# Loading the last groups of a streamed weight in other pieces: units of 16, 8, 4, 2, 1, 1 groups, whole but for the last

## The chip, the cores and the metric

One core of a Trainium2 chip. The metric is the device time of one execution in microseconds (us). Runs that are compared alternate on the same chip. Each trace is one execution; where a number is from one trace, the text says so.

## The reference

```python
# x [32, 256], y [32, 256], weight [128, 256, 256], all fp32
def reference(x, y, weight):
    return np.einsum('bi,bj,kij->bk', x, y, weight)
```

The weight is 33.55 MB and is used once. The rest is small.

## The kernel before

The 128 values of k are cut into 32 groups: group g has k = g, g+32, g+64, g+96. On one SBUF partition a group has eight rows of 256 values (a slice `ic` of i), which lie together in memory: 8 KiB of fp32. A load casts them to bf16, so that it writes 4 KiB for each partition and group. For each group, or two groups at once, TensorE adds eight matmuls (one for each `ic`) in PSUM, and VectorE multiplies by y and sums. Groups are worked on in units, and the table `LOADS` says which groups and which rows (from, to) each load brings, in the order of the queue.

```python
UNITS = (
    tuple(range(0, 32, 2)),      # 16 groups
    tuple(range(1, 32, 4)),      # 8
    (3, 11, 19, 27),
    (7, 23),
    (15, 31),
)
LOADS = (
    ((8, 24), 0, 8),
    ((4, 12, 20, 28), 0, 8),
    (tuple(range(2, 32, 4)), 0, 8),
    (tuple(range(1, 32, 4)), 0, 8),
    ((3, 11, 19, 27), 0, 8),
    ((7, 23), 4, 8),
    ((7, 23), 0, 4),
    ((15, 31), 0, 3),
    ((15, 31), 3, 5),
    ((15, 31), 5, 6),
    ((15,), 6, 8),
    ((31,), 6, 7),
    ((31,), 7, 8),
)
...
    for n, ((groups, lo, hi), s) in enumerate(zip(LOADS, s_w)):
        pool.dma_start(
            out=w_of(groups)[:, :, lo * J:hi * J],
            in_=rows_of(groups)[:, :, lo * J:hi * J],
        ).then_inc(s, 16)
...
    for u, unit in enumerate(UNITS):
        # matmuls of the unit, row by row; each waits for the load of its rows
        # then, on VectorE: one product and one sum for the unit
        # (the last unit: a fused product and sum for each group)
```

Groups 0 and 16 come as fp32 over another queue and are cast by ScalarE. All other loads of the weight are issued in the first 14 us and wait in one queue.

## Time and profile before

| | before |
|---|---|
| time, median of 3 (lowest, highest) | 86.06 us (86.01, 86.32) |
| span in the trace | 84.6 us |
| DMA, as the page's chain has it | 43% of the span, and the waits near the end |
| last piece of the weight has landed | 82.24 us |
| packets on the weight's queue | 5200 |

The page's slices (40 of 2.1 us, busy tenths) tell which engine is full at each time. The chain of work that ended last tells what set the end: a line of it is a start, a length and what ran or was waited for. The table of stretches gives, for a stretch of time, the busy time of each engine, TensorE's clock, the mean share of busy DMA engines and GB/s written. The prediction shows these lines.

Two more records are read below. A load adds 1 to its semaphore from each of the 16 DMA engines, so the trace has 16 times for each load: the middle one (between the eighth and the ninth) tells where the stream is, and I call the time from there to the sixteenth the **lag**. The packet records have a start, a size and a duration; a packet that took over 15 ns more than the usual time of its size (324 ns for 4096 bytes written, 173 for 2048, 98 for 1024, 60 for 512) I call **stretched**.

### The profile page before, as it was taken

The page shows a single profiled execution, that of the slowest core. Times are in us where ns is not written, and L with a number is a line of the kernel's source. Part 1 is how long each engine was busy: PE and PEld are TensorE (multiplying, and loading weights), DVE is VectorE, ACT ScalarE, POOL GpSimd, SP SyncE. Part 2 cuts the span into 40 slices and gives each one's busy share as a digit, 9 for nine tenths or more (in the row PEclk, how much of TensorE's full clock was granted, in tenths as well). Part 3 has the DMA queues.
Part 4 walks back from the last instruction along what each step waited for, and adds up shares of the span by engine and source line. Part 5 has one row for each costly group of instructions (what it writes and reads, how often), then busy time and mean ns, then how long its engine had stood idle before and what let it go on. Part 6 is the DMA issues. An engine that isn't in the chain of part 4 may idle for free.

```text
span 84.6 us, 277 instructions
## 1 busy us (share of the span) xinstructions
PE 32.4 (38%) x136; PEld 3.6 (4%) x38; DVE 24.9 (29%) x28; ACT 5.3 (6%) x5; POOL 10.7 (13%) x19
## 2 busy tenths in 40 slices
PE   0000000000000000000199999991079996985650
PEld 0000000000000000000000000000000010211110
DVE  0799600000000000000000000008999305999322
ACT  0638600000000000000000000000000000000000
POOL 0599994000000000000000000000000000000000
PEclk9999999999999999999999999999965999999995
DMA  4999999999999999999999999999999999999940
GB/s 112 387 411 258 211 213 217 215 213 217 213 215 211 215 217 217 215 217 215 211 215 217 215 213 217 215 215 215 209 217 217 217 215 202 208 206 207 187 53 8
DMA packets 5728, 17.91 MB, mean 212 GB/s; under 512 B 416, under 2 KB 1632, under 8 KB 5472
## 3 DMA queue, kind: packets, MB, share of 16 engines
q0 software_dynamic: 5200, 15.73, 94.5%
q1 hardware_dynamic: 432, 2.11, 6.6%
q10 hardware_dynamic: 96, 0.07, 0.3%
HBM read 33.62 MB, written 0.02 MB: 398 GB/s over the span
## 4 chain that ended last, share of the span: by engine, by line
DMA 43%; PE 38%; DVE 6%; another core or an unknown queue 4%; POOL 2%; issue 2%; POOLq 0%
DMA w_sb<-in_weight_dram 43%; PE ps L224 38%; DVE tmp L285 5%; POOL w_sb L150 1%; DVE tmp L294 0%; POOL ident L156 0%; POOL ident L155 0%; POOLq L134 0%; DVE acc L294 0%
## 5 line engine op out<-in xcount | busy, mean ns | idle before, releaser
L224 PE MATMUL ps<-w_sb,xblk 128*128 128x512 bf16 (+1 forms) x136 | 32.4, 393 | 50.3 <-DMA w_sb<-in_weight_dram 45.6
L285 DVE TENSOR_TENSOR tmp<-ps,y 128x4096 f32<-128x4096 f32 (+3 forms) x4 | 8.6, 2152 | 51.8 <-PE ps L224 51.8
L150 POOL DMA_DIRECT2D w_sb<-in_weight_dram x13 | 10.0, 778 | 2.6 <-POOLq L134 2.6
L289 DVE TENSOR_REDUCE acc<-tmp 128x16 f32<-128x4096 f32 (+3 forms) x4 | 8.6, 2154 | 0.1
L224 PEld LDWEIGHTS ps<-w_sb,xblk 128*128 128x128 bf16 x38 | 3.6, 100 | 78.7 <-DMA w_sb<-in_weight_dram 46.1
L165 ACT CAST w_sb<-w_f 128x1024 bf16<-128x1024 f32 x4 | 4.0, 1042 | 2.0 <-DMA w_f<-in_weight_dram 2.0
L294 DVE CUSTOM_DVE_ANT_0 tmp<-ps,y 128x256 f32<-128x256 f32 x2 | 0.8, 423 | 3.2 <-PE ps L224 3.2
L185 DVE STREAM_TRANSPOSE xt<-x_rep 32x256 f32<-32x256 f32 x4 | 1.7, 435 | 0.1
L214 DVE STREAM_TRANSPOSE y<-y_rep 32x256 f32<-32x256 f32 x4 | 1.7, 435 | 0.1
L197 DVE TENSOR_SCALAR xblk<-xt,mask 128x256 bf16<-128x256 f32 x4 | 1.5, 522 | 0.0
L179 DVE COPY x_rep<-x_sb 32x1024 f32<-32x1024 f32 x1 | 0.7, 681 | 2.6 <-PEq L134 2.6
L165 ACT ACT_TABLE_LOAD x1 | 1.3, 1283 | 2.6 <-PEq L134 2.6
L209 DVE COPY y_rep<-yt 32x1024 f32<-32x1024 f32 x1 | 0.7, 695 | 0.0
L206 DVE STREAM_TRANSPOSE yt<-y_sb 32x256 f32<-32x256 f32 x1 | 0.4, 422 | 0.0
L192 DVE TENSOR_REDUCE mask<-ident 128x4 f32<-128x128 f32 x1 | 0.4, 375 | 0.1
L156 POOL TENSOR_SCALAR_AFFINE_SELECT ident<-ident 128x128 f32<-128x128 f32 x1 | 0.3, 287 | 0.1
L155 POOL MEMSET ident<- 128x128 f32 x1 | 0.2, 223 | 0.0
L294 DVE DVE_READ_ACCUMULATOR2_ANT acc<- 128x1 f32 x2 | 0.2, 81 | 0.0
L324 POOL MEMSET const-float32-0.0<- 128x1 f32 x1 | 0.1, 98 | 0.2 <-issue 0.2
L324 POOL MEMSET const-bfloat16-1.0<- 128x1 bf16 x1 | 0.1, 102 | 0.0
L324 POOL MEMSET const-uint8-127<- 128x1 uint8 x1 | 0.1, 102 | 0.0
L324 POOL MEMSET const-float32-1.0<- 128x1 f32 x1 | 0.1, 98 | 0.0
## 6 DMA issues: line engine op xcount, KB each, us to landing
w_sb<-in_weight_dram POOLq DMA_DIRECT2D x2, 4096.0 KB, 46.1
w_sb<-in_weight_dram POOLq DMA_DIRECT2D x2, 2048.0 KB, 41.1
w_f<-in_weight_dram SPq DMA_DIRECT2D x2, 1024.0 KB, 6.3
w_sb<-in_weight_dram POOLq DMA_DIRECT2D x1, 1024.0 KB, 9.7
w_sb<-in_weight_dram POOLq DMA_DIRECT2D x2, 512.0 KB, 66.2
w_sb<-in_weight_dram POOLq DMA_DIRECT2D x1, 384.0 KB, 68.3
w_sb<-in_weight_dram POOLq DMA_DIRECT2D x1, 256.0 KB, 69.0
w_sb<-in_weight_dram POOLq DMA_DIRECT2D x2, 128.0 KB, 69.3
```

Source lines behind the costliest of these rows:

```text
L150: pool.dma_start(out=w_of(groups)[:, :, lo * J:hi * J], in_=rows_of(groups)[:, :, lo * J:hi * J],).then_inc(s, 16)
L165: c = act.copy(out=w_sb[:, place_of[g], lo:hi], in_=w_f[:, n, lo:hi])
L179: t = done(v.tensor_copy(out=x_rep, in_=x_sb.rearrange("b (ip ic) -> b ic ip", ic=IC).unsqueeze(3) .to_broadcast([B, IC, IP, KK]),)._wait_ ...
L185: c = v.transpose(out=xt[q * 32:(q + 1) * 32, :, :], in_=x_rep[:, :, q * IP // Q:(q + 1) * IP // Q, :],)
L192: t = done(v.tensor_reduce(out=mask, in_=ident.rearrange("p (ip kk) -> p kk ip", kk=KK), axis=AX, op=add,)._wait_ge(s_pool, 2))
L197: c = v.tensor_scalar(out=xblk[:, :, :, kk], in0=xt, scalar1=mask[:, kk:kk + 1], scalar2=None, op0=mult,)
L209: t = done(v.tensor_copy(out=y_rep, in_=yt.unsqueeze(3).to_broadcast([B, J // 32, B, KK]),)._wait_ge(s_dve, t))
L214: c = v.transpose(out=y4[q * 32:(q + 1) * 32, :].rearrange("p (jb j) -> p jb j", j=32), in_=y_rep[:, :, q * BQ:(q + 1) * BQ, :],)
L224: return pe.add_instruction(mybir.InstMatmult(name=nc.get_next_instruction_name(), engine=mybir.EngineType.PE, ins=[pe.lower_ap(rhs), pe.l ...
L285: t = done(v.tensor_tensor(out=prod, in0=sums, in1=y4.unsqueeze(1).to_broadcast([P, n_g, J]), op=mult,)._wait_ge(s_pe, n_pe))
L289: done(v.tensor_reduce(out=acc[:, unit[0]:unit[-1] + 1:unit[1] - unit[0]], in_=prod, axis=AX, op=add,)._wait_ge(s_dve, t))
L294: done(v.tensor_tensor_reduce(out=prod[:, n, :], in0=sums[:, n, :], in1=y4, scale=1.0, scalar=0.0, op0=mult, op1=add, accum_out=acc[:, g:g ...
```

## The change

Its intent: fewer and larger pieces at the end of the stream. Groups 7 and 23 come whole in one load. The pair (15, 31), which came in interleaved pieces, becomes two units: group 15 whole, and only group 31 in pieces, of 4, 2, 1 and 1 rows, so that little work is left after the last landing.

```diff
 UNITS
     (7, 23),
-    (15, 31),
+    (15,),
+    (31,),
 LOADS
-    ((7, 23), 4, 8),
-    ((7, 23), 0, 4),
-    ((15, 31), 0, 3),
-    ((15, 31), 3, 5),
-    ((15, 31), 5, 6),
-    ((15,), 6, 8),
+    ((7, 23), 0, 8),
+    ((15,), 0, 8),
+    ((31,), 0, 4),
+    ((31,), 4, 6),
     ((31,), 6, 7),
     ((31,), 7, 8),
 ... in the loop over units
-        n_b = n_g if last else n_g // 2
+        n_b = (n_g + 1) // 2
-        steps = [(ic, h, n_g // n_b * h) for ic in order for h in range(n_b)]
-        if last:
-            steps = steps[:12] + [(6, 0, 0), (7, 0, 0), (6, 1, 1), (7, 1, 1)]
+        steps = [(ic, h) for ic in order for h in range(n_b)]
-        if not last:
+        if n_g > 1:
             ... one product and one sum for the unit
         else:
-            for n, g in enumerate(unit):
-                ... fused product and sum of group g
+            ... fused product and sum of the unit's only group
 ... (bank and buffer places cut)
```

More of the change, by code (lines that the diff above doesn't have):

```diff
@@ L64 @@
     place_of = {g: i for i, g in enumerate(places)}
-    assert sorted(places) == list(range(G)) and len(UNITS[-1]) == 2 and B == 32
+    assert sorted(places) == list(range(G)) and len(UNITS[-1]) == 1 and B == 32
     def sbuf(name, shape, dtype):
@@ L241 @@
         n_g = len(unit)
-        last = u == len(UNITS) - 1
-        n_b = n_g if last else n_g // 2
+        n_b = (n_g + 1) // 2
         if bank + n_b > BANKS:
@@ L252 @@
         order = range(IC) if up else range(IC - 1, -1, -1)
-        steps = [(ic, h, n_g // n_b * h) for ic in order for h in range(n_b)]
-        if last:
-            steps = steps[:12] + [(6, 0, 0), (7, 0, 0), (6, 1, 1), (7, 1, 1)]
-        for n_step, (ic, h, o) in enumerate(steps):
+        steps = [(ic, h) for ic in order for h in range(n_b)]
+        for n_step, (ic, h) in enumerate(steps):
             n = n_g // n_b
+            o = n * h
             need = []
@@ L275 @@
                 c._wait_ge(need[-1], 16)
-            if n_step == len(steps) - 1 or (last and n_step == len(steps) - 3):
+            if n_step == len(steps) - 1:
                 n_pe += 1
                 c.then_inc(s_pe, 1)
-        prod = tmp[:, u % 2, :n_g, :]
-        if last:
-            sums = ps[:, bank:bank + n_g, 0, :]
-        else:
-            sums = ps[:, bank:bank + n_b, :, :].rearrange("p a h j -> p (a h) j")
-        if not last:
+        at = len(UNITS[1]) + u if n_g == 1 else 0
+        prod = tmp[:, u % 2 if n_g > 1 else 1, at:at + n_g, :]
+        sums = ps[:, bank:bank + n_b, :, :].rearrange("p a h j -> p (a h) j")[:, :n_g, :]
+        if n_g > 1:
             t = done(v.tensor_tensor(
@@ L292 @@
         else:
-            for n, g in enumerate(unit):
-                done(v.tensor_tensor_reduce(
-                    out=prod[:, n, :], in0=sums[:, n, :], in1=y4, scale=1.0, scalar=0.0,
-                    op0=mult, op1=add, accum_out=acc[:, g:g + 1],
-                )._wait_ge(s_pe, n_pe - 1 + n))
+            done(v.tensor_tensor_reduce(
+                out=prod[:, 0, :], in0=sums[:, 0, :], in1=y4, scale=1.0, scalar=0.0,
+                op0=mult, op1=add, accum_out=acc[:, unit[0]:unit[0] + 1],
+            )._wait_ge(s_pe, n_pe))
         bank += n_b
```

## The prediction

> **What bounds the kernel now.** I read the page's slices and queues first, then the chain of work that ended last, then a table of stretches cut at the landings of the last loads, and last the semaphore and packet records of the trace. The page of the kernel before has these lines (the span in 40 slices of 2.1 us; then the queue that carries the weight):
>
> ```profile
> PE   0000000000000000000199999991079996985650
> DMA  4999999999999999999999999999999999999940
> GB/s 112 387 411 258 211 213 217 215 213 217 213 215 211 215 217 217 215 217 215 211 215 217 215 213 217 215 215 215 209 217 217 217 215 202 208 206 207 187 53 8
> q0 software_dynamic: 5200, 15.73, 94.5%
> HBM read 33.62 MB, written 0.02 MB: 398 GB/s over the span
> ```
>
> The DMA engines are full from slice 1 to slice 37. The 215 GB/s count bytes written: the loads narrow fp32 to bf16, so the weight is read at twice that. TensorE starts halfway through and has holes. The time is therefore the time to stream 32 groups of 1 MiB, plus a short end. The chain confirms it for the end (start in us, length, what it was; "unknown queue" is the wait for a load):
>
> ```profile
> 71.36 4.48 PE ps L224 x20
> 75.83 0.46 another core or an unknown queue
> 76.29 0.05 issue
> ...
> 77.37 0.80 another core or an unknown queue
> ...
> 79.03 0.55 another core or an unknown queue
> ...
> 80.80 0.70 another core or an unknown queue
> 81.50 0.05 issue
> 81.55 0.63 PE ps L224 x3
> 82.18 0.06 another core or an unknown queue
> 82.24 0.05 issue
> 82.29 0.37 PE ps L224
> 82.66 0.02 issue
> 82.69 0.42 DVE tmp L294
> ```
>
> TensorE finishes what it has before the next piece lands, again and again, down to the last: the last piece lands at 82.24 us, and 2.36 us of fixed work (one matmul, one VectorE reduction, the store) follow to 84.6. So only the landing time of the last bytes matters. The table of stretches (window, us, busy times, TensorE clock, DMA share, GB/s written) shows that the stream slows before it ends:
>
> ```profile
> 61.50:71.30 9.80, 8.71 (x32) 0.78 (x7) 5.36 (x3) 0.00 (x0) 0.00 (x0) 0.83 1.06 213
> 71.30:76.30 5.00, 4.48 (x20) 0.97 (x10) 4.97 (x3) 0.00 (x0) 0.00 (x0) 1.00 1.13 209
> 76.30:78.20 1.90, 1.04 (x4) 0.31 (x4) 1.86 (x3) 0.00 (x0) 0.00 (x0) 1.00 1.17 204
> 78.20:79.60 1.40, 0.81 (x6) 0.19 (x2) 0.78 (x2) 0.00 (x0) 0.00 (x0) 1.00 1.32 191
> 79.60:80.40 0.80, 0.61 (x4) 0.19 (x2) 0.00 (x0) 0.00 (x0) 0.00 (x0) 1.00 1.26 180
> 80.40:80.80 0.40, 0.39 (x2) 0.10 (x1) 0.00 (x0) 0.00 (x0) 0.00 (x0) 1.00 1.38 163
> 80.80:82.20 1.40, 0.63 (x3) 0.21 (x3) 0.22 (x1) 0.00 (x0) 0.00 (x0) 1.00 0.24 31
> ```
>
> Whole groups go at 213 to 215, half groups at 209, three rows at 204, then 191, 180, 163. The last line is another thing: for 1.4 us only a quarter of the engines' time is used (0.24) while the kernel still waits. Some of the 16 engines are done and a few are late.
>
> **What the Trainium skill says.** "DMA: Bandwidth & Descriptors", section "Why small descriptors are slow (HBM only)", gives every packet a fixed overhead besides its bytes. The trace agrees that there is one: the median packet of 4096, 2048, 1536, 1024 and 512 written bytes took 324, 173, 135, 98 and 60 ns, which is about 22 ns plus 75 ns per KiB. Most of the 22 ns overlaps the next packet, since the share of busy engines is above 1 (1.06 to 1.38). The same page, section "Why a DMA increments its semaphore by 16 and not by 1", says that only the full 16 means that all has landed. The trace has 16 increments for each load, so the kernel pays the slowest engine every time; section "Latency and other measured facts" says that two of the engines are usually slower. The trace shows one increment always about 0.1 us behind the rest, but more than that at the end, below. "Rules for kernel authors" there asks for at least 1 MiB per DMA at full rate; here pieces of 128 KiB still come 0.36 us apart, because they are queued ahead.
>
> **The change part by part.** *Instructions.* The order of the built programs shows the same 120 matmuls of 512 columns, 16 of 256, and the same VectorE operations. Two DMA issues fewer (11 for 13) cost GpSimd 2 x 0.71 us (the median issue), all over by 13.7 us, long before they matter. Loads up to group 28, landed at 71.32, are untouched.
>
> *Packets.* One packet is one row piece of one group on one partition. Before, the last 4 groups took 512 + 768 + 384 = 1664 data packets, in 9 loads (the two halves of groups 7 and 23; three loads over two groups; three over one). After it is 256 + 128 + 4 x 128 = 896 in 6 loads. So 768 fewer, 48 per DMA engine. What 48 are worth comes from the time of the median engine. I take the middle of the 16 increments of each load: 71.03 (group 28), then 73.50, 75.97, 77.85, 79.16, 79.82, 80.46, 80.82, 81.18. The steps are 2.47 and 2.47 us (1 MiB in half groups), 1.88 (0.75 MiB), 1.31 (0.5 MiB), 0.66 (0.25 MiB in one-row packets), 0.64 (0.25 MiB in two-row packets), 0.36, 0.36 (0.125 MiB each). Sum 10.15. A MiB in whole rows takes 2.44: from 41.70 to 61.22 there are 8 of them. After: groups 7 and 23 whole, 2 x 2.44 = 4.88; group 15, 2.44; four rows of group 31, half of 2.47, 1.24; two rows, 0.64; one row twice, 0.72. Sum 9.92. **Saved on the median engine: 0.23 us**, on the path in full, since the chain ends in this stream.
>
> *The late engines.* The 16th increment lags the middle one by 0.28 us for the loads ending at 61.50 and 71.32, and by 0.32 at 78.17. Then 0.42, 0.54, 1.04, 1.03, 1.06 for the last five. So 0.76 us of the end is a lag that grew between 78.2 and 81.5. The packet records show where: between 79.3 and 79.9 us sixteen packets of 512 bytes took 87 to 246 ns instead of 60, and between 80.2 and 80.8 six of 1024 bytes took 251 to 405 instead of 98. Five increments slipped 0.4 us, and three of those slipped a further 0.4. Nothing in the trace names a cause. Nine packets of 2048 bytes were stretched likewise at 72.4 to 73.0 with no lasting lag. It happens where packets are small, and after the change each engine has 24 packets of at most 1024 bytes where it had 56 (16 + 16 + 8 + 8 + 8). I choose that half of the lag goes, 0.76 / 2 = 0.38, as a guess between nothing and all; a stretched packet among the last three pieces still hits.
>
> *TensorE and VectorE.* Two groups now start 8 matmuls at one landing instead of 4 and 4. With the saved time groups 7 and 23 land at about 76.2; their 8 matmuls take 8 x 0.224 (4.48 / 20) = 1.8 us, to 78.0. Group 15 lands at 78.6 and takes 8 x 0.135 (0.81 / 6) = 1.1, to 79.7. Group 31's first four rows land near 79.9, so TensorE waits again, and does them in 0.54. VectorE: product and sum of groups 7 and 23, 0.68 + 0.69, done by 79.5; one reduction of 0.42 + 0.08 for group 15, done by 80.3, before the last at 81.6. So neither joins the path, with about 0.2 us to spare at group 31's start and more later, as 1.1 us of matmul is left against 1.7 of stream. After the last landing the same 2.36 us follow.
>
> Sum: 0.23 + 0.38 = 0.6 us off 86.06, so **85.5 us**.
>
> **The rivals.** (1) *The lag stays:* the stretched packets come from something other than small packets, or the last three pieces alone bring them. For it: three of the five lagging loads keep their shape. Then 0.23 is saved, 85.8; and if the lag is worse, 86.1. (2) *The lag goes wholly:* 0.23 + 0.76 = 1.0, so 85.1. For it: loads of whole rows have kept to 0.28 throughout. Against it: the last three pieces are small still. (3) *TensorE becomes the bound*, because group 15's first matmul now waits for all eight rows. The sums above speak against it. A throttle would have to halve the clock over the last units: the page shows one such stretch of 3.4 us, before 66 us, and a second after 82. It would cost some 1 us of delay on work with 0.2 to 0.6 us of slack: at worst about 86.4. (4) *Hidden anyway*: if fewer packets freed nothing, because the memory side and not the packets limits the stream, 86.06 stays. The falling rates, 213 to 163, speak against it.
>
> **Range and chances.** The range runs from rival 2 with a little luck, 85.0, to the full lag with no gain, 86.05. A gain of 2% is 1.72 us; all that could be won is 0.39 (10.15 less 9.76) from packets and 0.76 from lag, 1.15 us, so faster has 2 in 100. Slower needs rival 3 doubled: 1 in 100.
>
> **What would show each step right or wrong.** Right: 4400 packets on the weight's queue (5200 less 768 and less 2 x 16 completions); groups 7 and 23 landing near 76.2 and group 15 near 78.7 to 78.8; a rate near 213 GB/s until then; last landing near 81.6, one matmul, one reduction, the store. Packet step wrong: the middle increments from group 28's landing to the end do not shorten by 0.2 to 0.3 us. Lag step wrong: the last increment trails the middle one by 1 us or more, or by 0.3. Wrong altogether: a chain that ends through matmuls one after another, without a wait for a load between them, or an early part of the stream that moved by more than the end did.

## The result, and the profile after

The changed kernel took 84.86 us (median of 4, 84.83 to 85.09), the kernel before 86.19 us in the same rounds (86.01 to 86.34). The ratio is 0.9852, 95% interval 0.9823 to 0.9882. A ratio here is the mean time of one kernel's runs over that of the other's of the same rounds, so it isn't quite the ratio of the medians. The prediction was 85.5 us, 85.0 to 86.05: the sign and the class (within 2%) were right, and the gain was about twice the one forecast, outside the range.

The page of the changed kernel, slices and the weight's queue:

```profile
PE   0000000000000000000089999995029999895780
DMA  3999999999999999999999999999999999999970
GB/s 86 408 396 285 216 216 206 216 218 216 216 216 212 212 218 214 218 218 216 206 216 214 220 216 216 212 212 218 214 218 218 212 210 216 214 218 218 193 111 8
q0 software_dynamic: 4400, 15.73, 94.1%
```

There are 800 packets fewer, as counted. Slices are counted from 0. From slice 4 to slice 36 the rate stays at 206 to 220 GB/s; before, it had fallen to 202 to 208 in slices 33 to 36 and then to 187 and 53. Now it is 193 and 111 in slices 37 and 38. The chain of the changed kernel, from group 28 on:

```profile
71.34 3.61 PE ps L223 x16
74.96 1.20 another core or an unknown queue
...
76.20 1.89 PE ps L223 x8
78.09 0.52 another core or an unknown queue
...
78.65 1.03 PE ps L223 x8
79.68 0.18 another core or an unknown queue
...
79.90 0.60 PE ps L223 x4
80.50 0.06 another core or an unknown queue
...
81.19 0.02 another core or an unknown queue
81.21 0.05 issue
81.26 0.30 PE ps L223
...
81.58 0.43 DVE tmp L288
```

It is the chain of before, with fewer and longer steps: TensorE still waits for each load, at last only briefly (0.06 and 0.02 us), and the last piece lands at 81.21 instead of 82.24. The table of stretches, cut at this kernel's landings:

```profile
71.30:76.10 4.80, 3.61 (x16) 0.68 (x7) 4.77 (x3) 0.00 (x0) 0.00 (x0) 1.00 1.07 216
76.10:78.60 2.50, 1.89 (x8) 0.68 (x7) 2.26 (x3) 0.00 (x0) 0.00 (x0) 1.00 1.03 203
79.90:80.50 0.60, 0.60 (x4) 0.29 (x3) 0.26 (x2) 0.00 (x0) 0.00 (x0) 1.00 1.32 174
80.50:81.20 0.70, 0.59 (x3) 0.21 (x3) 0.00 (x0) 0.00 (x0) 0.00 (x0) 1.00 0.23 29
```

The stretch in which only a quarter of the DMA engines' time is used has shrunk from 1.40 to 0.70 us. In the semaphore records, the lag is 0.33 to 0.38 us for every load from 42 us to the end, and no packet after 20 us is stretched (before: 33). So the 1.10 us between the two spans (84.61 and 83.51) is:

| from the two traces | before | after | saved, us |
|---|---|---|---|
| group 28's landing to the last, middle increments | 10.15 | 9.94 | 0.21 |
| position of the stream at group 28 (middle increment) | 71.03 | 70.93 | 0.10 |
| lag of the last load | 1.06 | 0.35 | 0.71 |
| last landing to the end of the span | 2.37 | 2.30 | 0.07 |

The last row is mostly the last matmul, 0.37 us before and 0.30 after: before, it fell where the clock was granted at 0.61 (mean of 82.2 to 83.0 us). In before_again, a second trace of that kernel, it took 0.30 as well, so this row is chance. The second row isn't the change's either: it lies before anything that was changed, and the second traces of the two kernels have 70.75 and 70.83 there. The result is 0.2 us more than these 1.1, because the kernel before varies from run to run, and the traced run of it (85.94 us) was a quick one (mean of the four untraced runs, 86.18).

### The profile page after: what moved, and what is told of

Its sections match the earlier page's. It is cut to its first block, busy times and chain, and to the rows that moved or that the text cites. A ratio compares the mean times of both kernels' runs of the same rounds, so it can differ in the third digit from the quotient of the medians.

```text
span 83.5 us, 280 instructions
## 1 busy us (share of the span) xinstructions
PE 32.3 (39%) x136; PEld 4.3 (5%) x43; DVE 25.0 (30%) x28; ACT 5.3 (6%) x5; POOL 8.9 (11%) x17
## 4 chain that ended last, share of the span: by engine, by line
DMA 44%; PE 39%; DVE 6%; another core or an unknown queue 3%; POOL 2%; issue 2%; POOLq 0%
DMA w_sb<-in_weight_dram 44%; PE ps L223 39%; DVE tmp L280 5%; POOL w_sb L149 1%; DVE tmp L288 1%; POOL ident L155 0%; POOL ident L154 0%; POOLq L133 0%; DVE acc L288 0%
## 5 line engine op out<-in xcount | busy, mean ns | idle before, releaser
L149 POOL DMA_DIRECT2D w_sb<-in_weight_dram x11 | 8.3, 764 | 2.6 <-POOLq L133 2.6
L223 PEld LDWEIGHTS ps<-w_sb,xblk 128*128 128x128 bf16 x43 | 4.3, 101 | 77.1 <-DMA w_sb<-in_weight_dram 42.8
```

The costliest lines, as they stand in the source:

```text
L149: pool.dma_start(out=w_of(groups)[:, :, lo * J:hi * J], in_=rows_of(groups)[:, :, lo * J:hi * J],).then_inc(s, 16)
L223: return pe.add_instruction(mybir.InstMatmult(name=nc.get_next_instruction_name(), engine=mybir.EngineType.PE, ins=[pe.lower_ap(rhs), pe.l ...
```

## The experiments

What I take as given: the loads set the end, and two thirds of the gain is lag. What isn't known: whether the loads alone do it, which of them, and what stretches packets. Theories: **A**, pieces of two groups in one load stretch packets; **B** (later C), the number of packets of less than a whole row does; **D**, a load that takes one row or few out of each eight. Rivals: the order of matmuls, the passing from one load to the next, packet size alone, or the work of other engines beside it. All 16 runs gave correct results. Their numbers stand together here; "late" counts stretched packets after 20 us, "small" is how many packets under 4096 bytes a DMA engine has.

| run | ratio to before | small | late, stretched | lag of the last load, us |
|---|---|---|---|---|
| the kernel before (first trace) | 1 | 104 | 33 | 1.06 |
| before_again | 0.9996 | 104 | 115 | 1.71 |
| split_pairs | 1.0016 | 104 | 41 | 1.10 |
| whole_7_23 | 0.9954 | 72 | 20 | 1.20 |
| halves_7_23 | 0.9882 | 64 | 18 | 0.85 |
| the changed kernel (first trace) | 0.9852 | 32 | 0 | 0.35 |
| after_again | 0.9855 | 32 | 1 | 0.26 |
| loads_only | 0.9849 | 32 | 0 | 0.28 |
| tail_6_2 | 0.9846 | 16 | 0 | 0.44 |
| many_whole | 0.9884 | 32 | 1 | 0.21 |
| singles_mid | 0.9876 | 32 | 0 | 0.48 |
| early_halves | 0.9874 | 160 | 12 | 0.36 |
| pad_15 | 0.9890 | 96 | 0 | 0.53 |
| tail_8x1 | 0.9915 | 64 | 50 | 0.39 |
| rows_15 | 1.0022 | 96 | 15 | 0.99 |
| rows_18_mid | 1.0134 | 96 | 64 | 0.85 |
| rows_12_early | 1.0179 | 96 | 0 (131 from 12 to 20 us) | 1.03 |
| stripes_15 | 1.0469 | 96 | 225 | 0.33 |

The 95% intervals of these ratios are about 0.003 to 0.005 to each side. The small ones of the changed kernel are the 32 of group 31.

**before_again: the kernel before, once more.** No edit.

> The kernel before, unchanged, as a second look at its trace. If the late DMA engines at the end belong to the kernel (theory: small pieces late in the weight stream bring stretched packets), stretched packets (more than 15 ns over the usual time of their size) come again in the last 4 us, some 15 to 25 of them, and the last increment of the last load trails the middle one by 0.8 to 1.2 us. If they were chance in one profile (rival), there are few or none and the lag is about 0.3 us. Time: within 0.3% of the kernel before, ratio 1.000.

The ratio was 0.9996 (0.9955 to 1.0036). The stretched packets came again, 115 of them, more than the 15 to 25 expected. 89 lie between 71.3 and 73.7 us, in the first half-row load of groups 7 and 23, which took 3.10 us on the middle engine instead of 2.47. The table of stretches of this trace has it, the second line against the first:

```profile
61.50:71.30 9.80, 7.85 (x26) 0.73 (x6) 6.26 (x2) 0.00 (x0) 0.00 (x0) 0.65 1.06 213
71.30:74.70 3.40, 3.40 (x17) 0.49 (x5) 1.73 (x1) 0.00 (x0) 0.00 (x0) 1.00 1.10 172
```

The rate falls to 172 GB/s, with the DMA engines as busy as ever (1.10): they hold packets longer. So stretching belongs to this kernel, but its place and size change from one execution to the next. The lag of 1.71 us was also more than the 0.8 to 1.2 expected. The kernel's time varies too: 86.31 to 87.54 us in 11 runs on this chip, against 85.10 to 85.48 in 6 of loads_only. That the stretching makes this variation is likely but not shown, as only two executions have a trace.

**loads_only: the loads of the change, the compute of before.**

```diff
 (the kernel before)
-LOADS = ( ... )
+LOADS = ( ... the changed kernel's ... )
```

> The loads of the changed kernel with the compute of the kernel before (groups 15 and 31 as one last unit, its matmuls interleaved). Theory that the loads do it all: ratio to before 0.985 (0.983 to 0.988), last landing near 81.2 us, no stretched packets. Rival that the order of matmuls or the reductions give a part of the 1.3 us: ratio 0.990 or more, and in it TensorE would end more than 0.6 us after the last landing.

Ratio 0.9849 (0.9806 to 0.9891), last landing at 81.19 us, no stretched packet: as the theory said. The new order of matmuls isn't needed for the gain. In the trace it only tidies the end: the chain of this run ends with two reductions on VectorE one after the other, at 81.50 and 81.93, so that VectorE ends 0.26 us later than in the changed kernel (82.27 against 82.01). Just before, 13 matmuls run from 79.88 to 81.47 us without a wait for a load: with the lag gone, TensorE is as late as the stream. At rounds on different chips the ratios (0.9849 and 0.9852) don't show this.

**whole_7_23 and halves_7_23: one part of the change alone, and the change without it.**

```diff
 whole_7_23 (the kernel before)          halves_7_23 (the changed kernel)
-    ((7, 23), 4, 8),                    -    ((7, 23), 0, 8),
-    ((7, 23), 0, 4),                    +    ((7, 23), 0, 4),
+    ((7, 23), 0, 8),                    +    ((7, 23), 4, 8),
```

> The kernel before with one edit: groups 7 and 23 come in one load of whole rows instead of two halves; 16 packets fewer an engine. If only packet overhead is saved there: 0.05 us (2 x 2.47 less 2 x 2.44), ratio 0.999. If the lag of late engines starts in these halves (nine packets were stretched there), it shrinks also at the end: up to 0.8 us, ratio 0.990. If stretched packets follow from the place in the queue (from about the 280th packet of each engine on), all shift by 17 places and part of the lag goes: ratio 0.994 to 0.998.

> The changed kernel with groups 7 and 23 again in two loads of four rows each (the rest of the change kept). If the pieces of groups 15 and 31 are the cause of the lag: ratio to before 0.986, the lag of the last load stays 0.3 us, 0.05 us lost against the changed kernel. If the halves start the lag: 0.990 to 0.995, stretched packets between 72 and 74 us and again at the end.

Groups 7 and 23 whole brought 0.9954 (0.9914 to 0.9995). The halves put back into the changed kernel gave 0.9882 (0.9836 to 0.9929), with 10 stretched packets at 75.2 to 75.6 us, at the end of the second half, a lag that stepped from 0.41 to 0.74 there and stayed near 0.85. That is earlier in the trace than the last pieces, but not the 72 to 74 us expected, and the time lies between the two expectations. Most of the gain comes with groups 15 and 31: halves_7_23 keeps 1.2 of the 1.5%. That the halves cost more than packet overhead (0.05 us, a ratio of 0.9994) fits both runs and the stretched packets, but isn't clear of the noise: the first interval reaches 0.9995, and the second overlaps that of loads_only. In the trace of halves_7_23 the clock was also granted at a half from 79.8 to 83.2 us, and the chain ends through 16 matmuls without a wait for a load, from 79.31 to 82.50. So in this one execution a last landing 0.66 us later than the changed kernel's (81.87 against 81.21) became 0.93 us at the end (82.94 against 82.01). An idea of mine on the side, stretching at a fixed place in the queue, fell too: of the two traces of the kernel before, one has most of it from an engine's 292nd packet on, the other at the 219th to 231st, and halves_7_23 has it at the 244th to 251st.

**split_pairs: pairs cut into single groups.**

```diff
 (the kernel before)
-    ((7, 23), 4, 8),
-    ((7, 23), 0, 4),
-    ((15, 31), 0, 3),
+    ((7,), 4, 8),
+    ((23,), 4, 8),
+    ((7,), 0, 4),
+    ((23,), 0, 4),
+    ((15,), 0, 3),
+    ((31,), 0, 3),
 (and so on for rows 3 to 5 and 5 to 6)
```

> The kernel before with each of its five loads that take pieces of two groups at once cut into two loads, one per group: same bytes, same packets (4992 of data), same row pieces, five loads more. Theory A (the stretched packets come from pieces of two groups in one load): no or few stretched packets, lag of the last load 0.3 to 0.5 us, ratio to before 0.990 to 0.993. Theory B (any load of less than whole rows stretches packets, so it is the number of small packets): stretched packets as before, lag 1 us or more, ratio 1.000 to 1.004.

Ratio 1.0016 (0.9974 to 1.0057), 41 stretched packets, lag 1.10. Theory A falls: it isn't the pair.

**early_halves, tail_8x1, tail_6_2: other pieces in the changed kernel.**

```diff
 early_halves
-    (tuple(range(2, 32, 4)), 0, 8),
+    (tuple(range(2, 32, 4)), 0, 4),
+    (tuple(range(2, 32, 4)), 4, 8),
 tail_8x1: group 31 in ((31,), 0, 1), ((31,), 1, 2) ... ((31,), 7, 8)
 tail_6_2: group 31 in ((31,), 0, 6), ((31,), 6, 8)
```

> The changed kernel with one early load, eight groups that are not waited for until 42 us, cut into two of half rows; 64 packets more on each engine, all of 2048 bytes. Plain packet cost: 8 MiB x 0.03 us = 0.24 us later, ratio to before 0.988. Theory B, or several groups in pieces as such: stretched packets between 22 and 42 us and a lag that grows there and stays to the end; ratio 0.992 or more. If only two groups 16 apart matter (their rows 4 MiB apart, here 1 MiB): no stretched packets.

> The changed kernel with group 31 in eight loads of one row each: 64 packets of 512 bytes an engine for that group instead of 32 of 512 to 2048 bytes. Theory A: no stretched packets; eight steps of 0.36 us from group 15's landing at 78.6 to 81.5, 0.3 us later than the changed kernel, ratio to before 0.988. Theory B: stretched packets among the 512-byte ones, lag 0.7 to 1 us, ratio 0.994 or more.

> The changed kernel with group 31 in two loads, of six and two rows. Last landing 0.1 us earlier (8 packets and two loads fewer an engine: about 16 x 5 ns), but after it two matmuls instead of one, 0.13 us more: no net gain, ratio to before 0.985 (0.983 to 0.988).

early_halves: 0.9874 (0.9844 to 0.9904), the plain packet cost and no more, although it has 128 more small packets on each engine (I had written 64, counting one half only). 12 packets were stretched, 9 of them whole-row packets just ahead of the first half. So theory B in its plain form, a count of small packets, falls as well: half rows of eight groups pass.

tail_8x1: 0.9915 (0.9885 to 0.9945), 50 stretched packets, but all at the start, in 1.1 us from 78.0: the first one-row load took 0.89 us on the middle engine, and the seven after it 0.34 to 0.36 as usual. The lag didn't grow (0.49 before this load, 0.39 after it): the loss sits in the middle increments here, and the lag alone wouldn't show it. The time lies between the two expectations, and theory A's "no stretched packets" fails.

tail_6_2: 0.9846 (0.9815 to 0.9877), no gain over the changed kernel (0.9852 and 0.9855), as expected.

**after_again, rows_15, many_whole, pad_15: what about a piece stretches packets.** The changed kernel once more, and three with one edit.

```diff
 rows_15: group 15 in ((15,), 7, 8), ((15,), 6, 7) ... ((15,), 0, 1)
 many_whole
-    (tuple(range(1, 32, 4)), 0, 8),
-    ((3, 11, 19, 27), 0, 8),
-    ((7, 23), 0, 8),
+    ((1,), 0, 8), ((5,), 0, 8), ... ((7,), 0, 8), ((23,), 0, 8),   # 14 loads
 pad_15: group 15's SBUF rows set 64 bytes apart, so that packets are cut at each row
+    w_15 = sbuf("w_15", [P, IC, J + 32], bf16)
+            for kk in range(KK):
+                pool.dma_start(
+                    out=w_15[kk:P:KK, :, :J],
+                    in_=weight[15 + G * kk].rearrange("(ip ic) j -> ip ic j", ic=IC),
+                ).then_inc(s, 16)
```

> The changed kernel once more, as a control for its missing stretched packets. If their absence belongs to the kernel: none or under five of them again, lag of the last load 0.3 to 0.5 us, ratio to before 0.985. If it was luck of one profile: 15 or more, lag 0.7 us or more.

> The changed kernel with group 15 in eight loads of one row each, on top of the pieces of group 31: 96 packets under 4096 bytes an engine instead of 32, 18 loads instead of 11, no pair in pieces. Plain packet cost: 8 x 0.36 = 2.88 us for the group instead of 2.44, so 0.44 us later, ratio to before 0.990. Theory C (stretching grows with the number of small packets late in the stream, whatever the groups): stretched packets come, ratio 0.994 to 1.002. Theory that it needs the old pieces of groups 7 and 23 or 15 and 31: none, ratio 0.990.

> The changed kernel with the last three loads of several groups cut into 14 loads of one whole group each: 22 loads instead of 11, the same data packets. If the changes from one load to the next stretch packets (completion writes, new rows), stretched packets appear between 42 and 76 us and the lag grows: ratio to before 0.990 or more. If only packets of part rows do: none, the 11 extra completion packets cost at most 11 x 22 ns = 0.24 us, ratio 0.985 to 0.988.

> The changed kernel with group 15 in packets of 512 bytes written, like the run with eight one-row loads, but each load reads its rows of the weight in one sequence (four loads of 32 partitions; the padded destination cuts the packets). Plain cost as there: 64 x 44 ns = 2.8 us for the group instead of 2.44, ratio to before 0.990. If packet size alone stretches packets: stretched packets as in that run. If it is reading one row in eight, over all partitions, at a stride: none here while there are some in that run.

after_again: 0.9855 (0.9826 to 0.9885), one stretched packet, lag 0.26: the quiet stream belongs to the changed kernel. many_whole: 0.9884 (0.9857 to 0.9910), lag 0.21, one stretched packet: 11 more loads of whole groups cost about 0.25 us (0.0029 of 86 us, within the intervals) and stretch next to nothing, so passing from load to load isn't the cause. rows_15 and pad_15 have the same 64 packets of 512 bytes an engine for group 15, and differ by 1.1 us in the mean of their runs: 1.0022 (0.9979 to 1.0066) against 0.9890 (0.9864 to 0.9916). rows_15 took back the whole gain of the change. The two traces show only a part of this, 0.44 us between their last landings (82.07 and 81.63), as the traced run of rows_15 was one of its quicker ones. The tables of the two, for the stretch of group 15 and the next, rows_15:

```profile
75.50:78.40 2.90, 2.19 (x13) 1.08 (x12) 2.87 (x4) 0.00 (x0) 0.00 (x0) 1.00 1.39 184
```

and pad_15:

```profile
75.50:78.40 2.90, 1.89 (x8) 0.68 (x7) 2.87 (x3) 0.00 (x0) 0.00 (x0) 1.00 1.41 194
```

Small packets are slower in both (184 and 194 instead of about 214); without stretched packets, as in pad_15, this is the packet cost of the prediction. Only in rows_15 was the lag driven up, from 0.50 to 0.86 and then 1.0. So packet size as written isn't enough; this left theory D, but pad_15 also used loads of 32 partitions. Another difference stays untested: the packet records give the bytes written, so whether pad_15 also reads one row at a time, or more at once, isn't known.

**stripes_15: loads of 32 partitions, yet one row at a time.**

```diff
+            for ic in range(IC - 1, -1, -1):
+                for kk in range(KK):
+                    pool.dma_start(
+                        out=w_sb[kk:P:KK, place_of[15], ic * J:(ic + 1) * J],
+                        in_=weight[15 + G * kk].rearrange("(ip ic) j -> ip ic j", ic=IC)[:, ic, :],
+                    ).then_inc(s, 16)
```

> The changed kernel with group 15 in 32 loads of 32 partitions and one row each, row by row: packets of 512 bytes as in pad_15 and rows_15, the order of reading of rows_15, the partitions of pad_15. Theory D (reading one row in eight at a time stretches packets): stretched packets after 75 us, a lag that grows by 0.3 us or more; with plain packets 0.44 us and some 24 x 22 ns = 0.5 us for completion writes, ratio to before 0.998 or more. Rival (loads of 32 partitions keep clear of it): no stretched packets, constant lag, ratio 0.992 to 0.997.

Ratio 1.0469 (1.0438 to 1.0500), 225 stretched packets, 219 of them from 75.6 us on, 31 us of excess in all engines together. The page's rates show the hole, in slices 34 to 37:

```profile
GB/s 115 415 410 228 215 208 221 217 210 214 214 215 217 215 212 217 215 217 208 217 215 215 214 214 214 221 214 212 214 219 217 208 215 217 124 138 139 101 0 7
```

Small loads of 32 partitions don't keep clear of it. In this run the lag was no measure (0.33): all engines were late alike. It also waits for 32 completions, and the end of its trace is TensorE's: the clock was granted at a half from 81.4 us on, and 16 matmuls follow group 15's landing (82.66) one after another for 3.58 us. The last landing is 2.3 us later than the changed kernel's (83.50 against 81.21), the end 4.7. So the size of its loss isn't all stretching.

**rows_12_early, rows_18_mid and singles_mid: one-row loads away from the end.** Group 12 in eight one-row loads at about 15 us; group 18 likewise at about 32 us; and the control of the latter, where the eight-group load is cut into whole groups only.

```diff
 rows_12_early
-    ((4, 12, 20, 28), 0, 8),
+    ((4,), 0, 8), ((12,), 7, 8), ((12,), 6, 7), ... ((12,), 0, 1), ((20,), 0, 8), ((28,), 0, 8),
 singles_mid
-    (tuple(range(2, 32, 4)), 0, 8),
+    ((2,), 0, 8), ((6,), 0, 8), ... ((30,), 0, 8),
 rows_18_mid: as singles_mid, with ((18,), 7, 8) ... ((18,), 0, 1) for ((18,), 0, 8)
```

> The changed kernel with group 12, which is read at about 15 to 20 us and first used at 42, in eight loads of one row. Plain packet cost 0.44 us in the stream plus a few completion writes: ratio to before 0.991. If the stretching belongs to the reading alone: stretched packets of 512 bytes there, and a lag that grows; ratio 0.994 or more. If it takes TensorE and VectorE at work beside it, or the end of the stream: none, ratio 0.990 to 0.992.

> The changed kernel with its eight-group load that is read from 22 to 42 us cut into eight loads of one whole group. Control: no stretched packets beyond a few, seven completion packets of 22 ns more, 0.15 us; ratio to before 0.987.

> The same, with group 18 (read at about 32 to 35 us) in eight loads of one row. If one-row loads stretch packets by themselves: stretched 512-byte packets at 32 to 35 us, a lag or a delay of all engines by some tenths of a us that stays to the end; ratio to before 0.994 or more, that is 0.3 us or more over the plain 0.44 us above the control (0.992). If it takes the work of the other engines beside it, or issues of GpSimd: none, ratio 0.991 to 0.993.

rows_12_early gave 1.0179 (1.0146 to 1.0213) and 131 stretched packets between 12 and 20 us, but GpSimd was still issuing loads there, to 17.6 us, so it didn't settle the question. rows_18_mid did. The control gave 0.9876 (0.9848 to 0.9905) and not one stretched packet. Eight one-row loads in it gave 1.0134 (1.0104 to 1.0164), 64 stretched packets between 31.6 and 34.3 us, and a lag of 0.8 us from there to the end. Between the two that is 2.2 us in time and 2.1 us in the last landing (83.49 against 81.37), where the plain packet cost is 0.44. The tables of stretches, the control first:

```profile
31.50:32.50 1.00, 0.16 (x1) 0.00 (x0) 0.00 (x0) 0.00 (x0) 0.00 (x0) 1.00 1.04 209
32.50:33.50 1.00, 0.42 (x1) 0.00 (x0) 0.00 (x0) 0.00 (x0) 0.00 (x0) 1.00 1.05 213
```

and rows_18_mid:

```profile
31.50:32.50 1.00, 0.23 (x1) 0.00 (x0) 0.00 (x0) 0.00 (x0) 0.00 (x0) 1.00 0.62 60
32.50:33.50 1.00, 0.35 (x1) 0.00 (x0) 0.00 (x0) 0.00 (x0) 0.00 (x0) 1.00 0.79 71
```

For two us the stream runs at a third of its rate, with VectorE, ScalarE and GpSimd idle and TensorE as little at work as in the control. The DMA engines themselves show gaps there (a share of 0.62 and 0.79), besides packets held longer. The first of the eight one-row loads took 1.57 us on the middle engine (31.91 to 33.48); the later ones 0.34 to 0.44. It takes neither the end of the stream nor work beside it. What it does take is shown only so far: loads of one row of each eight bring it, three times by a first load of that sort (0.89, 1.47 and 1.57 us in tail_8x1, rows_12_early and rows_18_mid, instead of 0.36; in rows_15 the first took only 0.42, and the lag grew later); loads of whole rows don't; packets of 512 bytes read in sequence didn't (pad_15); half rows of two groups do (before_again, halves_7_23), those of eight groups hardly (early_halves). It isn't the 8 MiB between the four k of a group: whole-row loads have it too, and stripes_15, which takes one k at a time, stretches without it. Whether the memory or the fetching of the packets' descriptors holds them up, no view of these traces tells. Nor is it clear why group 31's pieces in the changed kernel, after its half-row load, stay clean. The three long first loads come directly after whole rows, while the changed kernel steps down by four, two and one rows; but the first load of rows_15 comes directly after whole rows as well, so this is a guess that no run tests.

## Why the prediction was wrong, point by point

- **The bound** was right: the last landing sets the end. loads_only gets the whole gain with the old compute.
- **The packets.** 4400 on the queue, as said. The step of the middle engine was 0.23 us, measured 0.21 in the two traces.
- **TensorE and VectorE.** Right to 0.1 us so far as these: groups 7 and 23 landed at 76.16 (said 76.2), group 15 at 78.61 (78.6 in the working, 78.7 to 78.8 among the signs), group 31's first rows at 79.86 (79.9), with TensorE waiting for each of them, 0.18 us for the last (said 0.2). The "more later" was wrong: TensorE waited 0.06 and 0.02 us for the loads after that, because the stream ended earlier than predicted and the first four matmuls took longer (0.60 us for 0.54). Rival 3 didn't appear in the two traces of the changed kernel, but it was 0.02 us away, and in the trace of halves_7_23, at half the clock, it came.
- **The lag is the step that failed**: "I choose that half of the lag goes, 0.76 / 2 = 0.38, as a guess between nothing and all". All of it went: 0.71 us between the two traces, 0.35 left, which is what loads of whole rows have in that trace. It is the prediction's own sign of a wrong lag step, a trail of 1 us or more "or by 0.3". That the lag falls when these pieces go was right, and the term was mis-sized by about two: with no added lag the prediction's own steps give a last landing at 81.24 us (71.32 + 9.92), and it came at 81.21. This was rival 2, which was put at 85.1 us. The lag of before_again (1.71) and after_again (0.26) says the same.
- **What it rested on.** "It happens where packets are small" counted packets by size; as the reason for the lag this was wrong, or at least not enough. The runs show another thing: 128 small packets more on each engine cost only their overhead in early_halves, and 64 of 512 bytes only theirs in pad_15, while 64 of the same size, read one row of eight at a time, cost 1.1 us more in rows_15. The change took away the half-row loads of groups 7 and 23 and all pieces of group 15; what it left of part rows, group 31's, stays clean in both traces. Why it does is open.
- **The range.** It was cut at rival 2 "with a little luck". It took the lag of one trace, 1.06 us, for the kernel's. before_again had 1.71, so more could be won than the 1.15 us which the prediction called the most. The last matmul, 0.07 us shorter out of the slow clock, was not in the sum.
- **Hidden anyway** (rival 4) was wrong, by the 1.10 us between the spans.

## What to carry to other kernels

When a stream of loads sets the end, look at all 16 completions of the last loads and not at the rate alone: a gap between the middle one and the last is time that only some DMA engines need. As far as these runs show, cut a streamed tensor into whole contiguous rows wherever you can, and pay for part-row pieces only in the very last load or two, where they shorten the work after the landing. When a gain takes away a wait, look at what waits next: TensorE was 0.02 us from the end of the stream here. A term that varies between executions should be sized from several traces of the kernel before, not from one.

## What the Trainium skill lacked or had wrong

- "DMA: Bandwidth & Descriptors", "Why small descriptors are slow (HBM only)": a fixed overhead for each packet is there (22 ns in the packet's time, of which most overlaps), but no word that taking one row of each eight, 8 KiB apart, can hold the whole stream up. A first load of that sort took 1.57 us instead of 0.36 beside a nearly idle core (rows_18_mid), and the rate fell to 60 to 71 GB/s written from 209 to 213.
- The same page, "Rules for kernel authors", says that transfers under 64 KB are mostly overhead and asks for 1 MiB or more. No run here contradicts this. What it lacks is the cost for loads that wait in a queue: 14 loads of 1 MiB in place of three of 2 to 8 MiB cost about 0.25 us (many_whole), and the last loads, of 128 KiB read and 64 KiB written, land 0.36 us apart. That is 364 GB/s read against 430 for whole groups (1 MiB in 2.44 us). How loads cut the rows mattered more here than their size.
- The same page, "Latency and other measured facts", has engines that are usually slower. Here a lag of 0.2 to 0.5 us was there in every clean stream, but the large one, 0.8 to 1.7 us, came and went with the pieces, so a slower engine alone doesn't make it. Which engine was late, the records don't say.
- No page has that stretching varies between executions: 33 and 115 packets in two traces of one kernel, with its time from 85.69 to 87.54 us over all runs and chips (86.31 to 87.54 on one), and that of the changed kernel from 84.50 to 85.09 (84.50 to 84.95 on one).
